# Chunk states and C-by-state products from high and low float32r parts in a hybrid pooling and SSD block

## The chip, the cores and the metric

The kernel runs on one core of a Trainium2 chip. The metric is the device time of one execution in microseconds (us), as the median of several runs. The engines of the core work side by side, each through its own queue of instructions in order: TensorE (PE) does matrix products into PSUM, VectorE (DVE), ScalarE (ACT) and GpSimd (POOL) do elementwise work, and SyncE (SP) starts DMA transfers; ACT and POOL can start them too.

## The reference

One decoder block for 1024 tokens of width 1024, in float32: an adaLN norm, one input projection that feeds a pooling mixer and a Mamba-2 mixer (SSD), an output projection with a gated residual, then a squared-ReLU MLP with its gated residual and a final norm. The change touches only the SSD mixer, which works in 8 chunks of 128 tokens, with 16 heads of 64 columns in two groups of 8:

```python
scores = jnp.einsum('bclgn,bcsgn->bclsg', cc, bc)
y_diag = jnp.einsum('bclsgr,bcsgrp->bclgrp', scores[..., None] * decay_in, xdt)
states = jnp.einsum('bclgn,bclgr,bclgrp->bcgrpn', bc, decay_out, xdt)
...
def step(h, inp):
    st, dec = inp
    return h * dec[..., None, None] + st, h
...
y_off = jnp.einsum('bclgn,bcgrpn,bclgr->bclgrp', cc, prev, jnp.exp(a_cum))
return (y_diag + y_off).reshape(Bsz, S, G, R, P)
...
y = y.reshape(Bsz, S, SSD_INNER) * jax.nn.silu(z.astype(jnp.float32))
```

So each chunk and group makes a state (B transposed times the weighted x), adds it to the decayed state of the chunks before, and the next chunk multiplies its C by that state. The gate z multiplies the mixer's output.

## The kernel before

All of it is float32 arithmetic. Large products are made from two parts of each operand: the high part is the value cast to float32r, the low part is the value less its high part, and `mm3` (L239 to L247) adds three float32r products, high by high, high by low and low by high. All of these products have line L247 in the profile, whoever called them. The weights come in units (`unit`, L187): SP loads `raw` (L193), ACT makes `hi` (L198), DVE makes `lo` (L199).

The stages in order of time: a start-up with the adaLN products; from about 70 us `z0_tok` (L595), which makes the first 240 gate columns and the step sizes dt for each of the 8 token tiles, where ACT writes `zt` (L600, two buffers) and DVE writes the result into `z0s` (L601), a tile that stays in SBUF until the mixer's end; then rounds of `feat`, 24 products into one bank of PSUM, each followed by a causal convolution (`conv_half`: ACT L556, L565, L571 and DVE three times L568, then L576 or L579), whose results PE turns into token order later (L141). From 152 to 228 us these rounds carry head group 0 of the SSD: after every `feat` one closure from the `side` queue is emitted. From 241 us the rounds of the pooling mixer (`pool_half`, DVE L804 and L808) and the first rounds of the remaining gate columns (`z_tok`, L898) carry group 1 in the same way.

The closure of chunk c, called a step here, does the following. `ssd_a(c)`: PE makes the scores (L715); ACT makes eight tiles of decays (L724) from `R` into `dec`, a tile with four buffers; DVE multiplies them by the scores (L725); `ssd_x` makes `xdt` on DVE (L701) and, on POOL, `xw` (L705, one buffer) and the skip term into `tok` (L707); PE turns B (L141) and ACT copies it to `btok` (L733). `ssd_r(c+1)`: SP loads `R` (L691) and POOL masks it (L693). `ssd_b(c-1)`: PE multiplies C by the state into the bank `po` (L743), makes eight products of 64 columns into `py` (L746), and makes the chunk's state from `btok` and `xw` into `pst_` (L750). Then POOL decays the running state in place (L756) and DVE adds the new one (L757), and DVE adds up the output (L758, L761, L763) and, in group 0, multiplies by the gate from `z0s` (L765).

L743 and L750 are plain float32 products: a state of 128 by 512 and one matmul instruction each, which appears as two records in the trace. The state of chunk c-1 must be complete before L743 of the next step, which stands one `feat` later in PE's queue.

A scheduler fixes the order within each engine's queue from the order of emission and the waits between instructions; nothing overtakes in a queue when the kernel runs. PSUM has eight banks, given out in turn (`bank`).

Of the kernel before, what the change touches and what calls it, by code (L numbers as in the profile page):

```python
# [13 lines left out]
ALU = mybir.AluOpType  # L14
# [58 lines left out]
def tile_hybrid_block(  # L73
# [58 lines left out]
    cum_d = dramp.tile([2 * NT, S], F32, name="cum_d")  # L132
    ypool_d = dramp.tile([4, P, S], F32, name="ypool_d")
    hres_d = [dramp.tile([P, D], F32, name=f"hres{t}") for t in range(NT)]
    f_d = [dramp.tile([P, 2, 7, HW], F32, name=f"f_d{q}") for q in range(8)]
# [407 lines left out]
    carry = {ct: mp.tile([P, 4], F32, name=f"carry{ct}") for _, ct in G0}  # L543
    z0s = mp.tile([P, NT, Z0], F32, name="z0s")
    dtr = mp.tile([P, NT, HEADS], F32, name="dtr")
# [49 lines left out]
    def z0_tok(t, ks):  # L595
        ps = bank()
        tok_mm(ps[:, :256], t, ks)
        dve.tensor_tensor(out=dtr[:, t, :], in0=ps[:, Z0:256], in1=dtb, op=ALU.add)
        th = accp.tile([P, 272], F32, name="zt", tag="zt", bufs=2)
        act.activation(out=th[:, :Z0], in_=ps[:, :Z0], func=AF.Tanh, scale=0.5)  # L600
        dve.scalar_tensor_tensor(out=z0s[:, t, :], in0=th[:, :Z0], scalar=1.0, in1=ps[:, :Z0],  # L601
                                 op0=ALU.add, op1=ALU.mult)

    def feat(ks, h):
# [34 lines left out]

    ax, e_, s_, cumt = (mp.tile([P, HW], F32, name="dec", tag="dec", bufs=4)[:, :P] for _ in range(4))  # L640
    xf = dtr.rearrange("p t h -> p (t h)")
# [37 lines left out]
    live = {}  # L679
    states = {}  # L680

    def hbc(t, c_, g, n):
# [5 lines left out]
    def ssd_r(g, c_):  # L688
        a = c_ * HEADS + g * 8
        R = mp.tile([P, 8, P], F32, name="R", tag="R", bufs=2)  # L690
        sp.dma_start(out=R.rearrange("p h l -> p (h l)"),  # L691
                     in_=cum_d[a // 8:a // 8 + 1, :].broadcast_to([P, S]))
        pool.affine_select(out=R, in_=R, pattern=[[0, 8], [1, P]], compare_op=ALU.is_ge, fill=-1e38, base=0,  # L693
                           channel_multiplier=-1)
        Rs[(g, c_)] = R
# [15 lines left out]
    def ssd_a(g, c_):  # L711
        B, C = BC[8 + g], BC[10 + g]
        cs = slice(c_ * P, (c_ + 1) * P)
        pscore = bank()
        pe.matmul(pscore[:, :P], lhsT=B[:, cs], rhs=C[:, cs], start=True, stop=True)  # L715
        sc = pscore[:, :P]
        Ms = []
        R = Rs.pop((g, c_))
        for b in range(2):
            dec = mp.tile([P, HW], F32, name="dec", tag="dec", bufs=4)  # L720
            dv = dec.rearrange("p (h l) -> p h l", l=P)
            for i in range(4):
                a = c_ * HEADS + g * 8 + b * 4 + i
                act.activation(out=dv[:, i, :], in_=R[:, 4 * b + i, :], func=AF.Exp, bias=ncum[:, a:a + 1])  # L724
            dve.tensor_tensor(out=dv, in0=dv, in1=sc.unsqueeze(1).broadcast_to([P, 4, P]), op=ALU.mult)  # L725
            Ms.append(dec)
        xdt, xw = ssd_x(g, c_)
        btok = None
        if c_ < NT - 1:
            pb = bank()  # L730
            turn(pb[:, :P], B[:, cs])
            btok = mp.tile([P, P], F32, name="btok", tag="btok", bufs=2)
            act.copy(btok, pb[:, :P])  # L733
        live[(g, c_)] = (Ms, xdt, xw, btok)

    def ssd_b(g, c_):
        Ms, xdt, xw, btok = live.pop((g, c_))
        C = BC[10 + g]
        cs = slice(c_ * P, (c_ + 1) * P)
        yv = tok[:, c_, g * 512:(g + 1) * 512]  # L740
        if c_ > 0:
            po = bank()
            pe.matmul(po, lhsT=C[:, cs], rhs=states[g], start=True, stop=True)  # L743
        py = bank()
        for hh in range(8):
            pe.matmul(py[:, hh * HD:(hh + 1) * HD], lhsT=Ms[hh // 4][:, (hh % 4) * P:(hh % 4 + 1) * P],  # L746
                      rhs=xdt[:, hh * HD:(hh + 1) * HD], start=True, stop=True)
        if c_ < NT - 1:
            pst_ = bank()
            pe.matmul(pst_, lhsT=btok, rhs=xw, start=True, stop=True)  # L750
            if c_ == 0:
                states[g] = mp.tile([P, HW], F32, name="state", tag="state", bufs=1)
                act.copy(states[g], pst_)
            else:
                sv = states[g].rearrange("p (h d) -> p h d", d=HD)
                pool.tensor_tensor(out=sv, in0=sv, in1=hbc(cdec, c_, g, HD), op=ALU.mult)  # L756
                dve.tensor_tensor(out=states[g], in0=states[g], in1=pst_, op=ALU.add)  # L757
        dve.tensor_tensor(out=yv, in0=yv, in1=py, op=ALU.add)  # L758
        if c_ > 0:
# [4 lines left out]
        if g == 0:  # L764
            dve.scalar_tensor_tensor(out=tok[:, c_, 0:Z0], in0=tok[:, c_, 0:Z0], scalar=0.5, in1=z0s[:, c_, :],  # L765
                                     op0=ALU.mult, op1=ALU.mult)

    def queue_ssd(g):
        ssd_r(g, 0)
        for c_ in range(NT):  # L770
            def one(c_=c_):
                ssd_a(g, c_)
                if c_ + 1 < NT:
                    ssd_r(g, c_ + 1)
                if c_ > 0:
                    ssd_b(g, c_ - 1)
            side.append(one)
        side.append(lambda: ssd_b(g, NT - 1))
# [859 lines left out]
```

## Time and profile before

| what | value |
|---|---|
| median of 3 runs | 1151.14 us (1151.13 to 1153.94) |
| the profiled execution, its own time | 1152.16 us |
| its span | 1150.5 us |
| TensorE clock granted, mean of the span | 0.997 |
| DVE busy | 822.2 us (71%) |
| ACT busy | 562.6 us (49%) |
| POOL busy | 148.2 us (13%) |

The profile describes one execution. A busy time is the union of an engine's instructions, and an engine that waits in the middle of an instruction counts as busy. The chain of waits is followed back from the last instruction, so its rows give, in order of time, what the end waited for; "x24" in a row is the number of records merged into it. Rows of the windows view give the busy time of each engine within a stretch of the span.

### The profile page before, as it was taken

How to read it: one execution, taken by the hardware profiler on the slowest of the kernel's cores; microseconds unless marked ns; L12 is line 12 of the kernel's file. 1: busy time of each engine (PE TensorE's matmuls, PEld its weight loads, DVE VectorE, ACT ScalarE, POOL GpSimd, SP SyncE). 2: the span in 40 equal slices, each digit the busy share in tenths (PEclk: the TensorE clock that was granted, in tenths of full speed). 3: DMA queues.
4: the chain of work that ended last, by engine and by line, in shares of the span. 5: the costliest groups of instructions: out<-in, count | busy, mean ns of one | idle time of the engine just before them, and what ended most of it. 6: DMA issues, size and time to landing. Idle time of an engine off the chain costs nothing.

```text
span 1150.5 us, 15234 instructions
## 1 busy us (share of the span) xinstructions
PE 1138.3 (99%) x5541; PEld 948.1 (82%) x5541; DVE 822.2 (71%) x1230; ACT 562.6 (49%) x985; POOL 148.2 (13%) x188
## 2 busy tenths in 40 slices
PE   9999999999999999999999999999999999999997
PEld 9889887877898888888788888888888888888886
DVE  4769989967878667666987666665458744586985
ACT  4477575544354424545774444444434344434373
POOL 3011335425400012022000000000100000000030
PEclk9999999999999999999999999999999999999999
DMA  9932432223256656863165434342599835775832
GB/s 280 254 114 64 131 92 83 93 86 115 74 183 188 226 191 229 257 198 114 36 238 192 174 134 168 143 160 88 211 382 345 308 94 162 254 238 196 279 116 90
DMA packets 123899, 200.72 MB, mean 174 GB/s; under 512 B 8464, under 2 KB 65584, under 8 KB 121776
## 3 DMA queue, kind: packets, MB, share of 16 engines
q1 hardware_dynamic: 122464, 196.24, 50.9%
q0 software_dynamic: 1120, 3.21, 0.9%
q8 instruction: 43, 0.70, 0.3%
q10 hardware_dynamic: 240, 0.30, 0.1%
q14 instruction: 32, 0.26, 0.1%
HBM read 159.81 MB, written 39.91 MB: 174 GB/s over the span
## 4 chain that ended last, share of the span: by engine, by line
PE 79%; DVE 7%; DMA 7%; ACT 2%; issue 2%; POOL 1%; POOLq 0%; SPq 0%; DVEq 0%; ACTq 0%
PE bank L247 70%; DMA raw<-in_w_ada_dram 4%; PE bank L746 2%; DVE acc L854 2%; DMA raw<-ypool_d 1%; DMA raw<-in_w_out_dram 1%; DVE lo L199 1%; PE bank L141 1%; PE bank L750 1%; PE bank L338 1%; PE bank L743 1%; PE bank L821 1%; POOL rst L183 1%; POOL tok L1001 0%; DVE wx L1179 0%
## 5 line engine op out<-in xcount | busy, mean ns | idle before, releaser
L247 PE MATMUL bank<-u,hi 128*128 128x512 f32 x560 | 182.6, 405 | 0.5 <-ACT u L390 0.4
L247 PE MATMUL bank<-dlo,dhi 128*128 128x512 f32 (+1 forms) x464 | 177.2, 382 | 0.0
L247 PE MATMUL bank<-dhi 128*128 128x512 f32 (+1 forms) x464 | 177.2, 382 | 0.0
L247 PE MATMUL bank<-dhi,dlo 128*128 128x512 f32 (+1 forms) x464 | 177.1, 382 | 0.0
L1457 ACT CAST dhi<-fr 128x1024 fp32r<-128x1024 f32 x56 | 58.9, 1052 | 142.8 <-PE bank L247 109.1
L247 PEld LDWEIGHTS bank<-u,hi 128*128 128x128 f32 x560 | 103.7, 189 | 26.6 <-issue 4.8
L1458 DVE TENSOR_TENSOR dlo<-fr,dhi 128x1024 fp32r<-128x1024 f32 x56 | 68.4, 1222 | 78.6 <-ACT dhi L1457 77.9
L247 PE MATMUL bank<-hi,ym 128*128 128x512 f32 x384 | 123.6, 395 | 0.0
L247 PE MATMUL bank<-u,lo 128*128 128x512 f32 x280 | 110.2, 393 | 0.0
L198 ACT CAST hi<-raw 128x512 fp32r<-128x512 f32 (+2 forms) x101 | 62.9, 634 | 80.2 <-DMA raw<-in_w_out_dram 41.6
L247 PEld LDWEIGHTS bank<-dlo,dhi 128*128 128x128 f32 x464 | 87.2, 188 | 17.0
L247 PEld LDWEIGHTS bank<-dhi,dlo 128*128 128x128 f32 x464 | 87.2, 188 | 17.0
L247 PEld LDWEIGHTS bank<-dhi 128*128 128x128 f32 x464 | 87.2, 188 | 16.8
L199 DVE TENSOR_TENSOR lo<-raw,hi 128x512 fp32r<-128x512 f32 (+2 forms) x101 | 75.1, 752 | 30.3 <-ACT hi L198 29.9
L247 PE MATMUL bank<-E,whl 128*128 128x512 f32 x384 | 92.7, 391 | 0.1
L247 PEld LDWEIGHTS bank<-E,whl 128*128 128x128 f32 x384 | 71.7, 188 | 16.6 <-DVE whl L1231 0.9
L247 PEld LDWEIGHTS bank<-hi,ym 128*128 128x128 f32 x384 | 72.1, 188 | 14.8 <-ACT hi L198 0.2
L183 POOL TENSOR_TENSOR rst<-ssq,mhalf 128x1 f32<-128x1 f32 (+2 forms) x27 | 26.5, 984 | 401.7 <-DVE ssq L182 368.2
L247 PE MATMUL bank<-u,whl 128*128 128x512 f32 x312 | 75.6, 389 | 0.0
L247 PE MATMUL bank<-lo,ym 128*128 128x512 f32 x192 | 74.9, 390 | 0.2 <-DVE lo L199 0.2
L247 PEld LDWEIGHTS bank<-u,whl 128*128 128x128 f32 x312 | 58.5, 188 | 12.5 <-DVE whl L1231 0.5
L1231 DVE TENSOR_TENSOR whl<-wraw,whl 128x512 fp32r<-128x512 f32 x58 | 39.9, 688 | 38.4 <-ACT whl L1226 38.3
(272 smaller groups left out, 2144.9 us busy)
## 6 DMA issues: line engine op xcount, KB each, us to landing
f_d<-tok SPq DMA_DIRECT2D x16, 1792.0 KB, 7.1
wr<-in_w_down_dram SPq DMA_DIRECT2D x56, 512.0 KB, 5.6
fr<-f_d SPq DMA_DIRECT2D x53, 512.0 KB, 4.8
raw<-in_w_ada_dram SPq DMA_DIRECT2D x64, 256.0 KB, 2.9
wraw<-in_w_up_dram SPq DMA_DIRECT2D x15, 1024.0 KB, 5.3
raw<-in_w_in_dram SPq DMA_DIRECT2D x48, 256.0 KB, 3.1
raw<-in_w_out_dram SPq DMA_DIRECT2D x48, 256.0 KB, 3.1
tok<-in_x_dram SPq DMA_DIRECT2D x16, 512.0 KB, 6.4
```

The lines of the kernel that those rows point to most:

```text
L141: return pe.transpose(dst, src, ident)
L183: pool.tensor_tensor(out=rst[:, a:b], in0=m, in1=mhalf[:, :b - a], op=ALU.pow)
L198: act.copy(hi[:, :n], raw[:, :n])
L199: dve.tensor_tensor(out=lo[:, :n], in0=raw[:, :n], in1=hi[:, :n].bitcast(F32), op=ALU.subtract)
L247: pe.matmul(ps, lhsT=st_, rhs=mv, start=first and i == 0, stop=last and i == 2, skip_group_check=more)
L338: pe.matmul(warm_ps[:, 0:P], lhsT=ones, rhs=ones, start=True, stop=True)
L743: pe.matmul(po, lhsT=C[:, cs], rhs=states[g], start=True, stop=True)
L746: pe.matmul(py[:, hh * HD:(hh + 1) * HD], lhsT=Ms[hh // 4][:, (hh % 4) * P:(hh % 4 + 1) * P], rhs=xdt[:, hh * HD:(hh + 1) * HD], start=Tru ...
L854: dve.scalar_tensor_tensor(out=acc[0], in0=raw, scalar=cact[:, k:k + 1], in1=acc[0], op0=ALU.mult, op1=ALU.add)
L1231: dve.tensor_tensor(out=t_[:, 1], in0=src, in1=t_[:, 0].bitcast(F32), op=ALU.subtract)
L1457: act.copy(hi, src)
L1458: dve.tensor_tensor(out=lo, in0=src, in1=hi.bitcast(F32), op=ALU.subtract)
```

## The change

Five edits, all in the SSD stage and in what feeds it.

1. L743 and L750 become `mm3` calls with float32r parts: `shl` (state), `chl` (C of the chunk), `xhl` (the weighted x) and `bhl` (B of the chunk), each with one buffer. `two_parts` makes them: the high part by an ACT copy, the low part by a POOL subtraction. Per chunk and group these are two pairs of 128x512 and two of 128x128, seven times each per group.
2. The state's parts are made at the end of `ssd_b`'s state update, those of x, B and C at the end of the closure.
3. The decays are written over `R`, and the `dec` tiles are gone; `R` has three buffers in place of two, and the small temporaries of the step sizes lie in one of them.
4. `btok` has one buffer in place of two.
5. `z0s` is gone: DVE writes the first gate columns over `zt`, POOL's queue stores them to DRAM (`z0_d`), and SP loads them again into `z0` (two buffers) one chunk before they are used.

```diff
+    z0_d = [dramp.tile([P, Z0], F32, name=f"z0_d{t}") for t in range(NT)]
...
-    z0s = mp.tile([P, NT, Z0], F32, name="z0s")
...
         act.activation(out=th[:, :Z0], in_=ps[:, :Z0], func=AF.Tanh, scale=0.5)
-        dve.scalar_tensor_tensor(out=z0s[:, t, :], in0=th[:, :Z0], scalar=1.0, in1=ps[:, :Z0],
+        dve.scalar_tensor_tensor(out=th[:, :Z0], in0=th[:, :Z0], scalar=1.0, in1=ps[:, :Z0],
                                  op0=ALU.add, op1=ALU.mult)
+        pool.dma_start(out=z0_d[t], in_=th[:, :Z0])
...
-    ax, e_, s_, cumt = (mp.tile([P, HW], F32, name="dec", tag="dec", bufs=4)[:, :P] for _ in range(4))
+    dts = mp.tile([P, 8, P], F32, name="R", tag="R", bufs=3)
+    ax, e_, s_, cumt = (dts[:, i, :] for i in range(4))
...
-        R = mp.tile([P, 8, P], F32, name="R", tag="R", bufs=2)
+        R = mp.tile([P, 8, P], F32, name="R", tag="R", bufs=3)
...
         for b in range(2):
-            dec = mp.tile([P, HW], F32, name="dec", tag="dec", bufs=4)
-            dv = dec.rearrange("p (h l) -> p h l", l=P)
+            dv = R[:, 4 * b:4 * b + 4, :]
             for i in range(4):
                 a = c_ * HEADS + g * 8 + b * 4 + i
-                act.activation(out=dv[:, i, :], in_=R[:, 4 * b + i, :], func=AF.Exp, bias=ncum[:, a:a + 1])
+                act.activation(out=dv[:, i, :], in_=dv[:, i, :], func=AF.Exp, bias=ncum[:, a:a + 1])
...
-            btok = mp.tile([P, P], F32, name="btok", tag="btok", bufs=2)
+            btok = mp.tile([P, P], F32, name="btok", tag="btok", bufs=1)
...
+    def low_part(v, src):
+        pool.tensor_tensor(out=v[:, 1, :], in0=src, in1=v[:, 0, :].bitcast(F32), op=ALU.subtract)
+
+    def two_parts(name, src, n=HW):
+        v = mp.tile([P, 2, n], F32R, name=name, tag=name, bufs=1)
+        act.copy(v[:, 0, :], src)
+        low_part(v, src)
+        return v
...
             po = bank()
-            pe.matmul(po, lhsT=C[:, cs], rhs=states[g], start=True, stop=True)
+            shl, chl = shls[g], chls.pop((g, c_))
+            mm3(po, shl[:, 0, :], shl[:, 1, :], (chl[:, 0, :], chl[:, 1, :]), True, True, False)
...
             pst_ = bank()
-            pe.matmul(pst_, lhsT=btok, rhs=xw, start=True, stop=True)
+            xp, bp = xhl.pop((g, c_))
+            mm3(pst_, xp[:, 0, :], xp[:, 1, :], (bp[:, 0, :], bp[:, 1, :]), True, True, False)
...
+            shls[g] = two_parts("shl", states[g])
...
+                if g == 0:
+                    z0r[c_] = mp.tile([P, Z0], F32, name="z0", tag="z0", bufs=2)
+                    sp.dma_start(out=z0r[c_], in_=z0_d[c_])
                 if c_ > 0:
                     ssd_b(g, c_ - 1)
+                if c_ < NT - 1:
+                    xhl[(g, c_)] = two_parts("xhl", live[(g, c_)][2]), two_parts("bhl", live[(g, c_)][3], P)
+                if c_ > 0:
+                    chls[(g, c_)] = two_parts("chl", BC[10 + g][:, c_ * P:(c_ + 1) * P], P)
```

On PE, a step of group 0 stands in the queue before the change as follows (`ct` and `bt` are C and B in feature order, `u` and `hi` the operands of the `feat` that comes next):

```order
L715 MATMUL bank<-ct,bt 128x128
L141 MATMUL bank<-ident,bt 128x128
L743 MATMUL bank<-state,ct 128x512
L746 MATMUL bank<-xdt,dec 128x64 x8
L750 MATMUL bank<-xw,btok 128x512
L247 MATMUL bank<-u,hi 128x512 x2
```

And the same step on PE after it:

```order
L721 MATMUL bank<-ct,bt 128x128
L142 MATMUL bank<-ident,bt 128x128
L248 MATMUL bank<-shl,chl 128x512 x3
L759 MATMUL bank<-xdt,R 128x64 x8
L248 MATMUL bank<-xhl,bhl 128x512 x3
L248 MATMUL bank<-u,hi 128x512 x2
```

Nothing moved on PE; two instructions of each step became three float32r products each.

On POOL, one step of group 0 with the small copies of the convolution behind it, before:

```order
L756 TENSOR_TENSOR state<-state,cdec 128x512
L705 TENSOR_TENSOR xw<-tok,wdt 128x512
L707 TENSOR_TENSOR tok<-tok,dsk 128x512
L693 AFFINE_SELECT R<-R 128x1024
L561 COPY car<-craw 128x3
L563 COPY craw<-car 128x3
```

And one step on POOL after it:

```order
L742 TENSOR_TENSOR chl<-ct,chl 128x128
L742 TENSOR_TENSOR xhl<-xw,xhl 128x512
L742 TENSOR_TENSOR bhl<-btok,bhl 128x128
L711 TENSOR_TENSOR xw<-tok,wdt 128x512
L742 TENSOR_TENSOR shl<-state,shl 128x512
L770 TENSOR_TENSOR state<-state,cdec 128x512
L699 AFFINE_SELECT R<-R 128x1024
L713 TENSOR_TENSOR tok<-tok,dsk 128x512
```

Four subtractions are new in the step; that of the state stands behind those of x and B and behind the next chunk's `xw`.

On ACT, one step of group 0 from the copy of B on, before:

```order
L733 COPY btok<-bank 128x128
L724 ACTIVATE dec<-R,ncum 128x128 x8
L571 ACTIVATE craw<-cv 128x512
L198 CAST hi<-raw 128x512 x2
L556 COPY craw<-bank 128x512
L585 COPY tok<-bank 128x4x128
L565 ACTIVATE cv<-craw,pw 128x512
```

And one step on ACT after it:

```order
L738 COPY btok<-bank 128x128
L746 CAST chl<-ct 128x128
L729 ACTIVATE R<-R,ncum 128x128
L199 CAST hi<-raw 128x512
L746 CAST xhl<-xw 128x512
L746 CAST bhl<-btok 128x128
L746 CAST shl<-state 128x512
L571 ACTIVATE craw<-cv 128x512
L729 ACTIVATE R<-R,ncum 128x128 x7
L556 COPY craw<-bank 128x512
L585 COPY tok<-bank 128x4x128
L565 ACTIVATE cv<-craw,pw 128x512
```

Four casts are new, and seven of the eight decays moved behind the cast of the state and behind the convolution's tanh (L571).

More of the change, by code (lines that the diff above doesn't have):

```diff
@@ L680, in tile_hybrid_block @@
     states = {}
+    shls = {}
+    z0r = {}
+    xhl = {}
+    chls = {}
     def hbc(t, c_, g, n):
@@ L719, in ssd_a @@
         for b in range(2):
-            dec = mp.tile([P, HW], F32, name="dec", tag="dec", bufs=4)
-            dv = dec.rearrange("p (h l) -> p h l", l=P)
+            dv = R[:, 4 * b:4 * b + 4, :]
             for i in range(4):
                 a = c_ * HEADS + g * 8 + b * 4 + i
-                act.activation(out=dv[:, i, :], in_=R[:, 4 * b + i, :], func=AF.Exp, bias=ncum[:, a:a + 1])
+                act.activation(out=dv[:, i, :], in_=dv[:, i, :], func=AF.Exp, bias=ncum[:, a:a + 1])
             dve.tensor_tensor(out=dv, in0=dv, in1=sc.unsqueeze(1).broadcast_to([P, 4, P]), op=ALU.mult)
-            Ms.append(dec)
+            Ms += [dv[:, i, :] for i in range(4)]
         xdt, xw = ssd_x(g, c_)
@@ L731, in ssd_a @@
             turn(pb[:, :P], B[:, cs])
-            btok = mp.tile([P, P], F32, name="btok", tag="btok", bufs=2)
+            btok = mp.tile([P, P], F32, name="btok", tag="btok", bufs=1)
             act.copy(btok, pb[:, :P])
         live[(g, c_)] = (Ms, xdt, xw, btok)
+    def low_part(v, src):
[5 more added lines that the diff above has]
+        return v
     def ssd_b(g, c_):
         Ms, xdt, xw, btok = live.pop((g, c_))
-        C = BC[10 + g]
-        cs = slice(c_ * P, (c_ + 1) * P)
         yv = tok[:, c_, g * 512:(g + 1) * 512]
@@ L742, in ssd_b @@
             po = bank()
-            pe.matmul(po, lhsT=C[:, cs], rhs=states[g], start=True, stop=True)
+            shl, chl = shls[g], chls.pop((g, c_))
+            mm3(po, shl[:, 0, :], shl[:, 1, :], (chl[:, 0, :], chl[:, 1, :]), True, True, False)
         py = bank()
         for hh in range(8):
-            pe.matmul(py[:, hh * HD:(hh + 1) * HD], lhsT=Ms[hh // 4][:, (hh % 4) * P:(hh % 4 + 1) * P],
+            pe.matmul(py[:, hh * HD:(hh + 1) * HD], lhsT=Ms[hh],
                       rhs=xdt[:, hh * HD:(hh + 1) * HD], start=True, stop=True)
@@ L764, in ssd_b @@
         if g == 0:
-            dve.scalar_tensor_tensor(out=tok[:, c_, 0:Z0], in0=tok[:, c_, 0:Z0], scalar=0.5, in1=z0s[:, c_, :],
+            dve.scalar_tensor_tensor(out=tok[:, c_, 0:Z0], in0=tok[:, c_, 0:Z0], scalar=0.5, in1=z0r.pop(c_),
                                      op0=ALU.mult, op1=ALU.mult)
```

## The prediction

> **What bounds the kernel now.** I read the busy times of the page first, then the windows over the SSD stage, then the chain of waits inside it.
>
> ```profile
> PE 1138.3 (99%) x5541; PEld 948.1 (82%) x5541; DVE 822.2 (71%) x1230; ACT 562.6 (49%) x985; POOL 148.2 (13%) x188
> ...
> 170.00:180.00 10.00, 10.00 (x56) 8.01 (x55) 10.00 (x13) 5.26 (x15) 6.45 (x7) 1.00 0.21 69
> 180.00:190.00 10.00, 10.00 (x55) 8.01 (x55) 9.84 (x15) 6.29 (x17) 5.03 (x5) 1.00 0.30 93
> 280.00:290.00 10.00, 10.00 (x50) 7.63 (x49) 8.34 (x14) 3.88 (x11) 5.53 (x6) 1.00 0.33 116
> 300.00:310.00 10.00, 10.00 (x66) 8.09 (x64) 9.17 (x16) 5.25 (x15) 5.62 (x6) 1.00 0.00 0
> ```
>
> The columns of a window are its length, then PE, weight loads, DVE, ACT and POOL busy. PE is busy all the time at clock 1.00, so time taken from PE's queue shortens the run, as long as nobody keeps PE waiting. But in group 0 (170 to 190 us) DVE is as full as PE: 10.00 and 9.84 of 10. POOL's share of 13% of the span says little here; in these windows it is 5 to 6.5 of 10.
>
> The chain of waits runs through PE alone in this stretch; its rows give start, length and the work:
>
> ```profile
> 177.67 0.86 PE bank L743 x2
> 178.53 1.73 PE bank L746 x16
> 180.26 0.91 PE bank L750 x2
> 181.18 5.49 PE bank L247 x24
> 186.66 0.44 PE bank L141 x4
> ...
> 187.43 0.86 PE bank L743 x2
> ```
>
> One step of group 0 is 9.76 us (177.67 to 187.43), without a gap. From the end of L750 (181.18) to the next L743 there are 6.25 us, in which the state must be brought up to date.
>
> **What the change takes from PE.** The two lines have these records in all:
>
> ```profile
> L743 PE MATMUL bank<-state,ct x28: 592/593/595, 167.7 to 315.6; 128*128 128x512 f32 x28
> L750 PE MATMUL bank<-xw,btok x28: 592/620/648, 161.0 to 311.8; 128*128 128x512 f32 x28
> ```
>
> At two records each, that is 14 products per line. The 592 and 620 ns are lengths of overlapping records; what counts in a queue is the pitch, 0.86 and 0.91 in the chain. A float32r product of the same shape has a pitch of 5.49 / 24 = 0.229, so three cost 0.68. I leave the 0.05 by which L750 exceeds L743 on the new form, since it sits between the short products and the next work, not in the form: 0.73. The gain is 14 x (0.86 - 0.68) + 14 x (0.91 - 0.73) = **5.0 us**; it is 5.7 if the 0.05 goes and 4.3 if both lines carry it. Per step it is 0.36, so PE's step falls to 9.40 us.
>
> **What it adds to POOL, and through POOL to DVE.** These are the groups of POOL in 163 to 226 us, then those of DVE in 163 to 223 us, with the sum and the mean of one behind the bar:
>
> ```profile
> L707 POOL TENSOR_TENSOR tok<-tok,dsk 128x512 f32<-128x512 f32 x7 | 9.7, 1381 | 1.1 <-DVE xdt L701 0.6
> L693 POOL TENSOR_SCALAR_AFFINE_SELECT R<-R 128x1024 f32<-128x1024 f32 x7 | 9.4, 1347 | 14.7 <-DMA R<-cum_d 14.7
> L705 POOL TENSOR_TENSOR xw<-tok,wdt 128x512 f32<-128x512 f32 x6 | 8.0, 1336 | 9.5 <-PE bank L750 9.5
> L756 POOL TENSOR_TENSOR state<-state,cdec 128x512 f32<-128x512 f32 x6 | 6.3, 1045 | 4.1 <-PE bank L743 4.0
> L563 POOL COPY craw<-car 128x3 f32<-128x3 f32 x3 | 0.6, 187 | 0.2
> ...
> L568 DVE SCALAR_TENSOR_TENSOR cv<-craw,pw,cv 128x512 f32<-128x512 f32 x20 | 18.1, 907 | 0.0
> L763 DVE TENSOR_TENSOR tok<-tok,y 128x512 f32<-128x512 f32 x5 | 5.1, 1018 | 0.0
> L757 DVE TENSOR_TENSOR state<-state,bank 128x512 f32<-128x512 f32 x6 | 4.1, 680 | 0.0
> ```
>
> L763 and L757 are the same DVE operation on the same shape, but L757 reads one operand from PSUM and takes 680 ns, and L763 reads both from SBUF and takes 1018. The timeline shows why:
>
> ```profile
> 181.26 1.37 POOL L705 TENSOR_TENSOR xw<-tok,wdt 128x512 f32<-128x512 f32 x1 [1.59 <-PE bank L750]
> 182.70 1.37 POOL L707 TENSOR_TENSOR tok<-tok,dsk 128x512 f32<-128x512 f32 x1
> ...
> 181.64 0.68 DVE L757 TENSOR_TENSOR state<-state,bank 128x512 f32<-128x512 f32 x1
> 182.24 0.94 DVE L568 SCALAR_TENSOR_TENSOR cv<-craw,pw,cv 128x512 f32<-128x512 f32 x1
> 183.10 0.68 DVE L761 TENSOR_TENSOR y<-bank,ea 128x512 f32<-128x512 f32 x1
> 183.70 0.93 DVE L701 TENSOR_TENSOR xdt<-tok,dt 128x512 f32<-128x512 f32 x1
> ```
>
> L568, begun while `xw` still ran on POOL, is stretched to 0.94 and ends 0.55 us after `xw` does; POOL's L707 then takes 1.37 where L756 takes 1.05, and L701 in turn is stretched to 0.93. L757 and L761, with an operand in PSUM, run beside POOL at 0.68. So a DVE operation with both operands in SBUF and a POOL operation take turns. From the end of `xw` (182.63) to that of L707 (184.07), 1.44 us, one of each went through; DVE's pitch is 0.60 (181.64 to 182.24), which leaves 0.84 for one of POOL's.
>
> The Trainium skill, page "SBUF — State Buffer", section "SBUF: two separate sides", states this as a rule: GpSimd and a DVE operation with two SBUF inputs share one port pair, an exclusive lock held for the whole instruction. The trace agrees (1018 against 680 ns), and this is a rule that speaks against moving the low parts to GpSimd; what it gives if nothing softens it is the second rival below.
>
> Per step of group 0 DVE has, by the code, seven such operations (L568 three times, L579, L763, L701, and L199 about once) and the shorter L765: 7 x 0.60 + 0.3 = 4.5 us. POOL has four large ones and small copies: 4 x 0.84 + 0.2 = 3.6. Together that is 8.1 of the 9.76 us. The change adds two subtractions of 128x512, for which I take 0.84, and two of 128x128, which the trace doesn't show on POOL: between 0.19 (L563) and a whole one's 0.84, I take 0.35, a fixed 0.19 and a quarter of the rest. That is 2 x 0.84 + 2 x 0.35 = 2.4, and the sum 10.5 us against PE's 9.40. DVE has no free time in which to hide it.
>
> Group 0 has six steps with the full load, so the bound from strict turn-taking is 6 x 1.1 = 6.6 us of waiting on PE; the bound from below is 0, if the work fits between PE's demands after all. Some is absorbed: the last step's mask and skip term (two of POOL's, 2 us) may finish after the group, and the state has a little slack, worked out next. I take **4.0 us**, near the upper end, because the DVE rows say full.
>
> The slack: at the end of L750 the new queue of POOL still has the low parts of x and B, the next `xw` and then that of the state. ACT's part of it is priced by these groups (the copy of B and a cast of the same size):
>
> ```profile
> L733 ACT COPY btok<-bank 128x128 f32<-128x128 f32 x7 | 1.8, 258 | 0.0
> L198 ACT CAST hi<-raw 128x512 fp32r<-128x512 f32 x37 | 22.6, 619 | 42.8 <-DMA raw<-in_w_out_dram 37.8 <-PE bank L247 4.9
> ```
>
> A cast is 0.62, then POOL 1.05 + 0.35 + 1.05 + 1.05 and four gaps of 0.07: 4.4 us, or 5.6 with two turns given to DVE, of the 6.25 us. DVE's addition (0.68) and the cast of the state lie beside it. ACT itself gains 2 x 0.62 + 2 x 0.26 = 1.8 us per step on 5 to 6 of 10 and isn't full; but seven decays now stand behind the cast of the state in its queue, so a late state also delays the decays, DVE's multiplication by them and PE's products after that.
>
> **Group 1.** Its middle steps are longer and its windows less full (DVE 8.34, POOL 5.53 of 10): adding 2.4 to 3.2 us of POOL's work nearly fills the step. I take 1.2 us for four of them; bounds 0 and 3.2 (four times the 0.8 by which a sum made as above, 4.3 + 3.6 + 2.4 = 10.3, and the hand-overs may exceed 9.8). At the end the `feat` is shorter:
>
> ```profile
> 297.06 0.91 PE bank L750 x2
> 297.97 2.99 PE bank L247 x24
> ...
> 301.29 0.86 PE bank L743 x2
> ...
> 303.88 0.91 PE bank L750 x2
> 304.79 2.99 PE bank L247 x24
> ...
> 308.86 0.86 PE bank L743 x2
> ```
>
> From L750's end to the next L743 there are only 3.32 and 4.07 us, where the chain just priced needs 4.4 to 5.6. PE waits 1.1 + 0.3 = 1.4 to 2.3 + 1.5 = 3.8 us; DVE is at 9.17 of 10 there, so I take 3.0. Group 1 then costs **4.2 us**, bounds 1.4 and 7.0.
>
> **The gate columns by DRAM.** `zt` has two buffers and is now free only when POOL's transfer has landed:
>
> ```profile
> dtb<-in_dt_bias_dram POOLq DMA_DIRECT2D x1, 8.0 KB, 5.3
> ...
> 95.75 0.40 DVE L601 SCALAR_TENSOR_TENSOR z0s<-zt,bank 128x240 f32<-128x240 f32 x1
> ...
> 99.72 0.35 ACT L600 ACTIVATE zt<-bank 128x240 f32<-128x240 f32 x1
> ...
> 100.00:120.00 20.00, 20.00 (x98) 16.66 (x97) 19.90 (x44) 15.05 (x29) 2.17 (x5) 1.00 0.40 106
> ```
>
> Tile 4 is written by 96.15; with 5.3 us to land and some 0.6 to issue it frees its buffer at 102.0, and tile 6's tanh wants it at 99.72. ACT and, behind it, DVE lose up to 2.3 us, and DVE is full until 120. PE is covered by three units of weights made ahead, so I take **0.5 us**, bounds 0 and 2.3. The eight loads on SP and the third buffer of `R` I cost at nothing: a load is issued a chunk ahead of its use, and weights lie three units ahead behind it. Without that cover a late load would hold up the weights in SP's queue. The decays in place issue nothing new.
>
> **The sum.** -5.0 + 4.0 + 4.2 + 0.5 = +3.7 us. Against the profiled run's own time (span 1150.5, with 1.7 around it 1152.16) that is 1155.9; the median of the runs lies 1.0 lower, so **1154.8 us**.
>
> **Rivals.** First, the low parts are hidden (against the forecast, not slower): POOL's subtractions fall where DVE works on PSUM operands, and the state's low part is ready within the 6.25 us. It decides at the price of POOL's chain, 4.4 us without a turn for DVE. Then only the 1.4 us of the short steps remain: -5.0 + 1.4 = -3.6, 1147.5 us. For it: PE shows no gap anywhere in the stage before. Against it: DVE at 10.00 of 10. Second, strict turn-taking with nothing absorbed: -5.0 + 6.6 + 7.0 + 2.3 = +10.9, 1162.0 us. For it: both engines were stretched in nearly every step; against it: before the change buffers carried DVE through a full window without a gap on PE. Third, the waits come to about the gain and nothing measurable is left, 1151 us: the absorbed part is as large as the excess.
>
> **Chances.** The forecast, 1152 to 1158, has 0.40; the hidden case 0.18; the strict case 0.25; the even case 0.17. The range is 1146.8 to 1162.0: it takes in the hidden case with most of the gain's own bounds and ends at the strict one. A measurement can tell 0.3%, 3.5 us, from no change, so faster begins below 1147.7 and slower above 1154.6: 0.18 faster (the hidden case), 0.32 the same (the even case and a third of the forecast's), 0.50 slower.
>
> **What would show it.** In the profile after, three records of some 0.23 pitch in place of 0.86 and 0.91 confirm the gain. The term of group 0 shows as PE waiting on its state product for POOL's low part of the state, and as means of L568 and L763's successors above 907 and 1018 ns, with POOL near 8 of 10; that of the short steps as waits at 300 to 310 us. The gate term shows as ACT waiting at `zt` for a transfer. I am wrong if PE has no gaps in 160 to 320 us, or if the gaps end on something else, such as the decays on ACT or a load on SP.

## The result, and the profile after

The changed kernel takes **1189.84 us** (median of 5 runs, 1188.76 to 1193.04), the kernel before 1151.14 beside it: a ratio of 1.033 (95% interval 1.031 to 1.035). The prediction was 1154.8 with a range up to 1162.0, so it was 35 us too low: +38.7 us in place of +3.7.

The page of the kernel after, with its busy times and, in 40 equal slices, the clock granted to PE in tenths:

```profile
PE 1154.5 (97%) x5569; PEld 969.3 (82%) x5569; DVE 856.1 (72%) x1230; ACT 582.5 (49%) x1041; POOL 215.1 (18%) x252
...
PEclk9999998799879999999999999999999999999999
```

PE is busy 16 us longer although it has less to do, its clock has slices of 8 and 7, and POOL has 67 us more than before. The windows of the SSD stage show how that hangs together (length, then PE, weight loads, DVE, ACT and POOL busy, then PE's clock):

```profile
180.00:190.00 10.00, 9.06 (x30) 7.86 (x31) 10.00 (x11) 5.91 (x16) 8.64 (x10) 0.52 0.28 91
190.00:200.00 10.00, 10.00 (x58) 8.58 (x57) 9.54 (x10) 5.55 (x15) 7.12 (x8) 1.00 0.10 25
200.00:210.00 10.00, 7.71 (x38) 6.65 (x37) 10.00 (x11) 4.79 (x14) 9.43 (x8) 0.83 0.23 67
320.00:330.00 10.00, 6.42 (x21) 5.13 (x22) 7.22 (x11) 3.95 (x12) 5.37 (x5) 0.50 0.07 26
```

Before, PE filled every window of this stage at clock 1.00. Now it has holes, and behind some of them the clock stands at about a half. Where in the steps the time lies is told by PE's timeline: the sixteen short products of a step (L746 before, L759 after) mark its pace. Rows give start, length and the work; those of the kernel before are the second and the eighth of group 0:

```profile
168.60 1.89 PE L746 MATMUL bank<-xdt,dec 128*128 128x64 f32 x16
...
226.72 1.89 PE L746 MATMUL bank<-xdt,dec 128*128 128x64 f32 x16
```

```profile
167.45 1.89 PE L759 MATMUL bank<-xdt,R 128*128 128x64 f32 x16
...
181.96 3.51 PE L759 MATMUL bank<-xdt,R 128*128 128x64 f32 x16
...
243.28 1.89 PE L759 MATMUL bank<-xdt,R 128*128 128x64 f32 x16
```

Six steps took 58.12 us (226.72 - 168.60), 9.69 each; now they take 75.83, 12.64 each. The same starts, read from the timelines of all kernels of this study that the text uses, give this table (us; "between" is from the last of group 0 to the first of group 1, the middle of group 1 its first four steps, "short" its last three):

| kernel | step of group 0 | six steps | between | group 1, middle | group 1, short |
|---|---|---|---|---|---|
| before | 9.69 | 58.12 | 27.84 | 40.60 | 20.90 |
| after | 12.64 | 75.83 | 30.58 | 53.49 | 28.19 |
| e4, float32 products | 9.69 | 58.12 | 29.10 | 41.01 | 20.97 |
| e6, e4 + unread subtractions | 12.27 | 73.63 | 35.79 | 50.37 | 23.19 |
| e16, e6 + decays behind | 10.84 | 65.04 | 28.57 | 44.80 | 24.84 |
| e9, after without y1 | 11.78 | 70.68 | 32.32 | 52.88 | 26.33 |
| e15, after + decays behind | 11.34 | 68.01 | 29.08 | 46.52 | 29.74 |
| e22, e15 without y1 | 10.45 | 62.72 | 28.44 | 44.89 | 29.06 |
| e2, after without low parts | 9.72 | 58.34 | 31.12 | 41.09 | 19.89 |
| e23, e2 + decays behind | 9.40 | 56.38 | 27.83 | 39.54 | 19.88 |

From the second step of group 0 to the end of group 1 the kernel after needs 188.1 us and the one before 147.5: the difference, 40.6 us, is the whole loss and a little more. The start-up with the gate columns costs nothing that shows (the second step begins at 167.45 where it began at 168.60).

What the engines wait for in 160 to 350 us (in all, times, longest):

```profile
ACT R L729 <- POOL R L699: 50.0, 13, 6.8
...
DVE psum L826 <- ACT craw L822: 19.5, 6, 8.8
POOL xhl L742 <- ACT xhl L746: 18.1, 10, 7.1
...
PE bank L843 <- issue: 9.9, 2, 7.1
PE bank L248 <- POOL shl L742: 9.3, 5, 3.1
```

Before, ACT never waited for POOL's mask of `R` there. Now that is the largest wait. What PE waits for is small beside it: the low part of the state, 9.3 us, and in group 1 the pooling mixer's product (L843), 9.9 us. For the second the profile names no releaser ("issue"), but its 7.1 us end at 323.58, just when DVE has made `pp` (L835, 322.43 to 323.48). DVE's `psum` in turn waits for ACT's copy `craw` (L822), which at 312.85 stands behind seven decays that had waited 6.48 us for the mask. The chain of waits through one step of group 0 shows how such a wait comes about:

```profile
182.43 2.15 ACT R L729 x7
...
185.53 0.72 ACT cv L565
186.90 0.63 ACT xhl L746
187.59 1.55 POOL xhl L742
189.15 0.86 POOL bhl L742
190.01 1.00 POOL xw L711
191.01 1.71 POOL shl L742
192.80 1.37 POOL state L770
194.17 1.51 POOL R L699
195.70 2.16 ACT R L729 x7
```

The mask ends at 182.43 and lets ACT do the decays; the convolution's `cv`, the casts, POOL's low parts, the next `xw`, the low part of the state and the update of the state follow, and behind them in POOL's queue stands the next mask, which ends at 195.70. One such **turn** is 13.3 us here, four of them (182.43 to 231.91) take 12.4 on average, near the step of 12.64, and PE isn't in it.

POOL's groups in 165 to 245 us (busy, mean ns of one, idle before):

```profile
L742 POOL TENSOR_TENSOR shl<-state,shl 128x512 fp32r<-128x512 f32 x7 | 11.2, 1596 | 3.0 <-ACT shl L746 3.0
...
L742 POOL TENSOR_TENSOR xhl<-xw,xhl 128x512 fp32r<-128x512 f32 x5 | 7.5, 1507 | 3.0 <-ACT xhl L746 3.0
...
L742 POOL TENSOR_TENSOR bhl<-btok,bhl 128x128 fp32r<-128x128 f32 x6 | 5.1, 858 | 0.0
L742 POOL TENSOR_TENSOR chl<-ct,chl 128x128 fp32r<-128x128 f32 x6 | 3.8, 635 | 9.3 <-ACT chl L746 9.3
```

And DVE's in 165 to 240 us:

```profile
L568 DVE SCALAR_TENSOR_TENSOR cv<-craw,pw,cv 128x512 f32<-128x512 f32 x19 | 18.6, 978 | 2.3 <-ACT cv L565 2.3
...
L778 DVE TENSOR_TENSOR tok<-tok,y 128x512 f32<-128x512 f32 x5 | 8.2, 1646 | 0.0
L730 DVE TENSOR_TENSOR R<-R,bank 128x512 f32<-128x512 f32 x12 | 7.6, 675 | 0.0
```

A low part of 128x512 occupies POOL for 1.5 to 1.6 us and one of 128x128 for 0.6 to 0.9. DVE's operations with both operands in SBUF went from 907 to 978 ns (L568) and from 1018 to 1646 (L778, which was L763), while L730, with one operand in PSUM, stays at 675.

### The profile page after: what moved, and what is told of

Same layout as the page of the kernel before. It is cut to its first block, busy times and chain, and to the rows that moved or that the text cites. A ratio compares the mean times of both kernels' runs of the same rounds, so it can differ in the third digit from the quotient of the medians.

```text
span 1188.2 us, 15455 instructions
## 1 busy us (share of the span) xinstructions
PE 1154.5 (97%) x5569; PEld 969.3 (82%) x5569; DVE 856.1 (72%) x1230; ACT 582.5 (49%) x1041; POOL 215.1 (18%) x252
## 4 chain that ended last, share of the span: by engine, by line
PE 70%; POOL 6%; ACT 6%; DVE 2%; issue 2%; DMA 1%; POOLq 0%; SPq 0%; ACTq 0%; DVEq 0%
PE bank L248 67%; ACT R L729 2%; POOL shl L742 1%; POOL R L699 1%; POOL xhl L742 1%; PE bank L759 1%; POOL xw L711 1%; DMA R<-cum_d 1%; PE bank L142 1%; ACT cv L565 1%; PE bank L843 0%; POOL bhl L742 0%; POOL state L770 0%; ACT xhl L746 0%; ACT craw L556 0%
## 5 line engine op out<-in xcount | busy, mean ns | idle before, releaser
L200 DVE TENSOR_TENSOR lo<-raw,hi 128x512 fp32r<-128x512 f32 (+2 forms) x101 | 82.5, 825 | 30.0 <-ACT hi L199 30.0
```

Of the source, the lines that this page charges most:

```text
L200: dve.tensor_tensor(out=lo[:, :n], in0=raw[:, :n], in1=hi[:, :n].bitcast(F32), op=ALU.subtract)
```

## The experiments

Two reasons stood first: the **loop theory** (the turn just shown sets the step) against the **full VectorE** or **load theory** (POOL's added time and DVE's turns with it set it). VectorE is DVE, GpSimd POOL, ScalarE ACT and TensorE PE in the expectations.

### Which of the edits

e4 puts the products back and keeps the rest of the change, but for `btok`, which has its two buffers again (in e6, e10, e12 and e16 too):

```diff
-            mm3(po, shl[:, 0, :], shl[:, 1, :], (chl[:, 0, :], chl[:, 1, :]), True, True, False)
+            pe.matmul(po, lhsT=BC[10 + g][:, c_ * P:(c_ + 1) * P], rhs=states[g], start=True, stop=True)
...
-            mm3(pst_, xp[:, 0, :], xp[:, 1, :], (bp[:, 0, :], bp[:, 1, :]), True, True, False)
+            pe.matmul(pst_, lhsT=btok, rhs=xw, start=True, stop=True)
```

> Changed kernel with the two products back in plain float32 (no casts, no low parts); first gate columns through DRAM, decays in place and three buffers of R stay. Loop and full VectorE theory alike: these edits cost nothing, 1149 to 1154 us. If the in-place decays or the loads of the gate columns carry a part of the loss: above 1160.

Measured: 1154.12 us, ratio 1.0008 (0.9992 to 1.0023). By themselves the gate columns through DRAM and the decays in place cost nothing. The single buffer of `btok` isn't in this run.

e6 adds to e4 four POOL subtractions in each step, at the places of the change, of the same sizes, into a tile that nobody reads:

```diff
+    def extra(a, b):
+        pool.tensor_tensor(out=xtra[:, :a.shape[1]], in0=a, in1=b, op=ALU.subtract)
...
+            extra(states[g], BC[8 + g][:, :HW])
```

> The kernel of the run before (float32 products) with GpSimd subtractions of the same four shapes and at the same four places a step, whose results nobody reads: the load on GpSimd and on the memory that it shares with VectorE is that of the change, but no cast stands before them and nobody waits for them. Loop theory: near the kernel without them, 1150 to 1158 us. Full VectorE theory: VectorE's two-operand instructions stretch by some 2.7 us a step in group 0 and less in group 1, 1168 to 1190 us.

Measured: 1187.02 us, ratio 1.029 (1.0258 to 1.0322). **Nearly the whole loss comes back with plain float32 products, no casts, and nobody reading the results.** The load theory's number held, and my loop, which ran through the casts, had predicted no loss. But e6's own chain shows a turn, of 12.4 us, without casts:

```profile
219.92 1.51 POOL R L699
221.46 2.17 ACT R L729 x7
224.57 0.72 ACT cv L565
...
226.64 0.74 DVE cv L568
227.38 0.61 DVE state L769
228.06 1.72 POOL xtra L784
...
232.31 1.51 POOL R L699
```

Mask, decays on ACT, `cv` behind them, DVE's convolution, DVE's new state behind that, POOL's subtraction that waits for that state, and behind it the next mask. An unread result still holds up what stands behind it in its queue.

### The order of the decays

What joins these queues is the place of the decays on ACT. The order of the two programs, with the numbers of buffers, at the fifth chunk of group 0 (its `R` is 2043 before and 2089 after; the copy and `cv` belong to the same half of the convolution in both):

```
before: L556 COPY craw_2002<-bank_1977 128x512
        L585 COPY tok_66<-bank_2014 128x4x128
        L565 ACTIVATE cv_2007<-craw_2002,pw_117 128x512
        L733 COPY btok_2041<-bank_2039 128x128
        L724 ACTIVATE dec_2111<-R_2043,ncum_825 128x128 x4
        L724 ACTIVATE dec_2117<-R_2043,ncum_825 128x128 x4
after:  L729 ACTIVATE R_2089<-R_2089,ncum_832 128x128 x7
        L556 COPY craw_2050<-bank_2025 128x512
        L585 COPY tok_66<-bank_2062 128x4x128
        L565 ACTIVATE cv_2055<-craw_2050,pw_125 128x512
        L738 COPY btok_2087<-bank_2085 128x128
```

Before, the decays needed one of four `dec` tiles and stood behind the convolution. In place, with a third buffer of `R`, they need only the mask, and the scheduler has put them ahead of the convolution, which now waits for the mask with them. (That the missing wait moved them is read from the order; no run undid this edit alone.) Three runs force the old place: e16 on e6, e15 on the kernel after, and e20, which puts the decays behind the casts of x and B as well.

```diff
+        marks.append(nc.cur_bb.bb.instructions[-1])      # cv in group 0, craw in group 1
...
                 act.activation(out=dv[:, i, :], in_=dv[:, i, :], func=AF.Exp, bias=ncum[:, a:a + 1])
+                tc.add_manual_dep(nc.cur_bb.bb.instructions[-1], marks[-2].name, ...)
```

> The kernel with float32 products and unread GpSimd subtractions, with one thing forced: on ScalarE a chunk's decays stand behind the convolution's three instructions (copy, token copy, cv) of the step before, as in the kernel before; with decays in place they had moved ahead of them. Every instruction stays. Order theory (mask behind GpSimd's instruction on the new state, decays behind the mask, convolution behind the decays on ScalarE, new state behind the convolution on VectorE: 12.3 us a turn): broken, 1150 to 1166 us. Load theory (GpSimd's added time and VectorE's turns with it are the limit): 1182 to 1191 us.

> The changed kernel with the decays on ScalarE forced behind the convolution's three instructions of the step before. Order theory: the turn over the convolution and the state is broken; the casts of xw and B still stand behind four to eight decays, so a turn over the cast of xw remains, about 11 us: 1155 to 1175 us. Load theory: 1184 to 1192 us.

> The changed kernel with the decays forced behind the convolution's instructions and behind the casts of C, xw and B of the chunk before. Order theory: no instruction of ScalarE that GpSimd waits for is behind the mask; only GpSimd's own 10.5 us a step is left, 1150 to 1168 us. Load theory: 1184 to 1192 us.

Measured: e16 1170.74 (ratio 1.0147, 1.0129 to 1.0164), e15 1176.38 (1.0194, 1.0174 to 1.0214), e20 1180.74 (1.0222, 1.0186 to 1.0259). All three lie between what the two theories gave. So the order is a cause: forcing it gives back 16 of e6's 33 us and, in e15, 13 to 16 of the 39. It is not the only one, and putting the decays further back gained nothing more. The scheduler also moved a few other instructions with the decays: PE's order is the same in e15 as in the kernel after, but on POOL the mask now stands more often ahead of the product that decays the state. So these 13 to 16 us belong to the forced order as a whole.

Two runs had tried to break the turn by moving the mask instead: e1 places it ahead of the low parts of C, x and B in POOL's queue, e10 gives e6 a fourth buffer of `R` and emits the masks one chunk earlier.

```diff
+                with pinned((pool,)):
+                    if c_ + 2 < NT:
+                        ssd_r(g, c_ + 2)
```

> Changed kernel, but GpSimd's mask of R for chunk c+2 is placed ahead of the low parts of chunk c in its queue (with three buffers of R its load then waits for chunk c-1's products). Loop theory (mask behind low parts behind casts behind decays behind mask, 13 us a turn): the loop is cut, the step falls from about 12.8 to what GpSimd's own work takes, 10.5 us, over some 12 steps: 1162 to 1172 us. Full VectorE theory (VectorE had 98% of each step before, and the low parts lengthen its two-operand instructions by 2.7 us a step): the same work remains, 1184 to 1192. Clock theory: if the PE waits stay, so does the half clock, 1184 to 1192; if they go, below 1165.

> The kernel with float32 products and unread GpSimd subtractions, with a fourth buffer of R, so that GpSimd's masks run one chunk further ahead; every instruction of GpSimd, VectorE, ScalarE and PE is kept. Loop theory, now without the casts (a GpSimd instruction that needs the new state stands ahead of the mask, the mask ahead of the decays on ScalarE, these ahead of the convolution that VectorE does before it makes the next state): a mask that is a chunk early breaks it, 1150 to 1162 us. Load theory (GpSimd's 10.5 us a step and VectorE's turns with it are themselves the limit): 1180 to 1191 us.

Measured: e1 1180.19 (1.0239, 1.0206 to 1.0272), e10 1186.12 (1.0302, 1.0276 to 1.0328). I first took e10 for the end of the loop theory. But in its order the scheduler had moved the decays one chunk ahead together with the masks, so that ACT still ran straight behind each mask: e10 didn't test what it was meant to, though its time is the load theory's. In e1 the mask still stood behind the low part of the state, and its time lies between what the two theories gave. Both are inconclusive.

### Half of the low parts

e11 keeps only the chunk states from parts, e12 only C by state, e13 has all of the change but makes the state's low part on DVE, and e21 is e11 with the decays behind the convolution and the casts.

> Changed kernel with only the chunk states from high and low parts (low parts of xw and of B, GpSimd); C by state is a plain float32 product. Loop theory: nothing ahead of the mask needs the state, the turn over the cast of xw takes 10.5 us or less, 1149 to 1160 us. Load theory: half of the added GpSimd work, half of the loss, 1166 to 1174 us.

> Changed kernel with only C by state from high and low parts (low parts of the state and of C, GpSimd); the chunk states are plain float32 products. Same number and sizes of GpSimd instructions as in the run with the chunk states only. Loop theory: the low part of the state stands ahead of the mask, so the loop over VectorE's state remains, 11 to 12 us a turn, 1166 to 1182 us, well above the other half. Load theory: the same as the other half, 1166 to 1174 us.

> Changed kernel with the low part of the state alone made by VectorE (0.68 us where L200 had no partner), the other three low parts by GpSimd. Loop theory: the state leaves GpSimd's queue, 1153 to 1166 us. Load theory: GpSimd loses one of its two long low parts, VectorE gets it, 1174 to 1186 us.

> The kernel with only the chunk states from high and low parts, with the decays forced behind the convolution's instructions and behind the casts of xw and B. Order theory: 1146 to 1153 us, the kernel before less half of TensorE's 5 us or level with it. Load theory: no better than without the forced order, 1163 to 1169 us.

Measured: e11 1167.66 (1.0143, 1.0119 to 1.0167), e12 1171.89 (1.0187, 1.0159 to 1.0216), e13 1177.36 (1.023, 1.0202 to 1.0258), e21 1155.94 (1.0034, 1.0014 to 1.0053). Either half of the low parts brings about half of the loss, and e13 too lies where the load theory had it. Yet in e11 the order makes most of that half: e21 does all that e11 does and is 1.1% of the time, 12 us, nearer to the kernel before, where the load theory saw no change. It ends some 3 us above the range of the order theory.

### DVE's work, alone and with the order

e9 takes 2.2 us of DVE's work from each step (`y1` and its addition), e22 does so in e15, and e3 gives all low parts to DVE.

```diff
-            dve.tensor_tensor(out=y1.rearrange("p (h d) -> p h d", d=HD),
-                              in0=po.rearrange("p (h d) -> p h d", d=HD), in1=hbc(ea, c_, g, HD), op=ALU.mult)
-            dve.tensor_tensor(out=yv, in0=yv, in1=y1, op=ALU.add)
+            dve.tensor_copy(out=y1[:, 0:4], in_=po[:, 0:4])
```

> Changed kernel without VectorE's product of C by state with ea and without its addition to the token values (L776, L778: the contribution of earlier chunks is left out of the result), 0.68 and 1.49 us of VectorE a step; a copy of four columns frees the bank. GpSimd, ScalarE and PE do all they did. Loop theory: these are not in the loop, 1183 to 1191 us. Full VectorE theory: each step falls by about 2.2 us, fourteen times, 1158 to 1170 us.

> The changed kernel with both edits that alone gave little: the decays on ScalarE behind the convolution's instructions, and VectorE without the product of C by state with ea and its addition (the contribution of earlier chunks is left out of the result). Two-limits theory (the turn through GpSimd, ScalarE and VectorE's state, 12.5 us, and VectorE's own stretched step, 11.6 us, both stand above TensorE's 9.4 us, so that lifting one shows the other): together they give far more than the 13 and 3 us of each alone, 1147 to 1158 us. GpSimd's own time as the limit: 1168 to 1176 us, the sum of the two at best.

> The changed kernel with all four low parts made by VectorE instead of GpSimd (quiet 0.68 us for 128x512, some 0.2 for 128x128: 1.8 us a step). Two-limits theory: GpSimd is back at its time of before and the turn over it is short, but VectorE, which had 0.2 us of a step free, gets 1.8 us, in group 0 alone some 1.4 us a step over and less in group 1: 1158 to 1172 us. If GpSimd's time alone is the limit: 1146 to 1152 us.

Measured: e9 1186.44 (1.0292, 1.0263 to 1.0322), e22 1168.60 (1.0151, 1.0132 to 1.017), e3 1176.28 (1.0215, 1.0192 to 1.0238). The step of group 0 gives back 0.86 us of the 2.2 in the one order (12.64 to 11.78) and 0.89 in the other (11.34 to 10.45). So DVE isn't the limit that the full VectorE theory took it for, and my idea of two limits of which one hides the other falls too, since the two edits simply add up. e22's chain runs mostly through POOL:

```profile
191.66 1.45 POOL state L775
193.15 0.83 POOL chl L747
...
196.11 1.00 POOL xw L714
197.11 1.84 issue
...
198.99 1.45 POOL shl L747
...
203.35 1.04 POOL state L775
```

From `state` at 191.66 to the next `state` at 203.35 it is 11.7 us. e22's time is what its expectation gave for GpSimd's own time as the limit (1168 to 1176 us), but that reason isn't shown: the 1.84 us that the chain calls "issue" are a wait. POOL's timeline of e22 names what ended it, and the group of the same instruction in e15 (165 to 240 us) has six of them with 10.6 us of idle time before them:

```profile
198.99 1.45 POOL L747 TENSOR_TENSOR shl<-state,shl 128x512 fp32r<-128x512 f32 x1 [1.88 <-ACT shl L751]
```

```profile
L747 POOL TENSOR_TENSOR shl<-state,shl 128x512 fp32r<-128x512 f32 x6 | 8.2, 1360 | 10.6 <-ACT shl L751 10.6
```

So POOL waits for ACT's cast of the state, and that cast (198.29 in e22) had waited 3.81 us for DVE's new state (L776, 197.59), which stands in DVE's queue behind two instructions of the convolution of 1.01 and 1.35 us (0.74 for the third). So read, POOL makes DVE's state late, and the late state makes POOL wait: the two set the step together. In e22, with less work on DVE, such waits of POOL add up to 6.8 us in 160 to 350 us; in e15 they are 12.7. And e3, with POOL's load gone and 1.8 us more on DVE, has steps of 11.93 and a time above both of its expected ranges, so DVE could not have taken the low parts either.

One window of 165 to 235 us of e15, and then of e22, shows how little a busy share tells here:

```profile
165.00:235.00 70.00, 65.78 (x332) 55.53 (x330) 69.77 (x78) 40.66 (x103) 56.57 (x56) 0.90 0.25 77
```

```profile
165.00:235.00 70.00, 66.22 (x358) 55.97 (x357) 69.63 (x82) 42.39 (x105) 60.83 (x59) 0.98 0.29 88
```

DVE is at 69.8 of 70 us in the one and at 69.6 in the other, though 2.2 us were taken from each of its steps: an instruction that waits for its turn with POOL counts as busy.

### Without the low parts

e2 drops the four subtractions and lets the products take the high parts twice; e23 is the same with the decays behind the convolution.

```diff
-        low_part(v, src)
...
-            mm3(po, shl[:, 0, :], shl[:, 1, :], (chl[:, 0, :], chl[:, 1, :]), True, True, False)
+            mm3(po, shl[:, 0, :], shl[:, 0, :], (chl[:, 0, :], chl[:, 0, :]), True, True, False)
```

> The changed kernel without the four subtractions on GpSimd; the products take the high parts twice, so that TensorE and ScalarE do what they did (the low parts of state, C, xw and B are left out of the result). Two-limits theory: GpSimd is back at its time of before, VectorE is no longer stretched, and the casts alone hold nobody up, 1145 to 1151 us. If the casts on ScalarE are a part of the loss: above 1156 us.

> The changed kernel without the four subtractions (products take the high parts twice, the low parts are left out of the result) and with the decays forced behind the convolution's instructions: the most that the shorter products can bring, if low parts cost nothing. If the order ate TensorE's 5 us in the run without low parts: 1145 to 1148 us. If VectorE, with 98% of a step of group 0, lets no shorter step pass there: only group 1 can gain, 1148 to 1152 us.

Measured: e2 1154.07 (1.0031, 1.0017 to 1.0044), e23 1146.99 (0.996, 0.9947 to 0.9974). e2 lies between its two expected ranges: the casts and PE's shorter products alone, in the new order, are no gain; in the old order they bring 4.6 us. That is PE's 5.0 within the interval, and the long steps of group 0, 9.76 us before, take 9.40. PE's and POOL's instructions stand in the same order in both runs, so the difference between them, 8 us, is the order on ACT and what moved with it on DVE and SP. DVE reads as full as ever in e23 (60 us of it):

```profile
165.00:225.00 60.00, 60.00 (x336) 51.66 (x335) 59.42 (x76) 38.99 (x100) 31.07 (x32) 1.00 0.30 90
```

### PE's halved clock

e26 puts the sixteen short products ahead of the product of C by state, so that PE has work where it waited.

```diff
+        with pinned((pe,)):
+            py = bank()
...
+            if c_ > 0:
+                po = bank()
```

> The changed kernel with TensorE's sixteen short products of a step forced ahead of the product of C by state, so that TensorE has 1.73 us of work where it waited for the state's low part. Two-limits theory: other engines set the step, TensorE's waits and the halved clock after them are hidden, 1184 to 1192 us. Clock theory (a wait of 3 us costs 3 to 10 us more at a granted clock of 0.5): fewer halved stretches and 1165 to 1180 us.

Measured: 1189.91 us (1.0335, 1.0308 to 1.0363). Two windows of the kernel after, then the same of e26 (PE's clock is the figure behind the five engines):

```profile
160.00:250.00 90.00, 82.02 (x389) 69.51 (x388) 86.21 (x96) 50.49 (x127) 64.66 (x62) 0.87 0.28 82
270.00:350.00 80.00, 67.76 (x328) 56.68 (x326) 55.95 (x77) 33.02 (x90) 52.36 (x49) 0.85 0.21 68
```

```profile
160.00:250.00 90.00, 79.78 (x408) 67.14 (x407) 87.35 (x101) 51.43 (x131) 62.09 (x63) 0.92 0.28 82
270.00:350.00 80.00, 68.56 (x343) 57.14 (x341) 58.42 (x82) 32.93 (x90) 51.04 (x48) 0.89 0.24 75
```

The clock rose from 0.87 to 0.92 and from 0.85 to 0.89: of 90 and 80 us, by estimate, 23.7 us had been lost to it (0.13 x 90 + 0.15 x 80) and now 16.0 are, and the time stayed. So far as this run shows, PE's slow stretches are a follower here: they fill time in which others set the step.

No kernel of these that takes a product from high and low parts, with all of the work in it, beats the kernel before; e21 comes nearest, 0.3% above it.

## Why the prediction was wrong

- **PE's gain, -5.0 us: right.** Three records in place of two, and 9.40 us for the long steps, as predicted; e23 shows -4.6 (-3.0 to -6.1).
- **"The decays in place issue nothing new", cost 0: the step that failed first.** They issue nothing, but they lost their wait for a `dec` tile, and with it their place behind the convolution. The prediction quoted the new order, read it as decays moved *behind* the cast of the state, and named a late state that delays the decays, without asking what stands behind the decays. They were the next chunk's, moved *ahead* of the convolution. The order costs nothing with float32 products (e4), 8 us with casts and no low parts (e2 less e23, 1.0031 - 0.996), and 16 us with low parts (after less e15, 1.0332 - 1.0194). The other part of the error is larger: the low parts themselves cost 27 us in the old order (e15 less e23, 1.0194 - 0.996), where 8.2 were counted, 4.0 for group 0 and 4.2 for group 1.
- **The slack of the state: right as a sum, wrong as a question.** POOL's 4.4 to 5.6 us of 6.25 were priced as one pass. The mask at the end of that pass and the decays that need it make it a turn, and a turn is compared with the step: 12.4 on average against 9.40.
- **Group 0, +4.0 (bounds 0 and 6.6).** Against the 56.38 us of e23 the six steps took 19.4 more. From after to e15 the order is 7.8 of them (75.83 - 68.01), and e15's 11.6 over e23 are the low parts themselves, with a step of 11.34 us. The prediction counted 10.5 for strict turn-taking and called it an upper bound. It left out that POOL's queue has waits of its own, above all that for the cast of a state which DVE brings late (10.6 us in e15's group 0), and that DVE's operations on PSUM, five with a pitch of 0.6 us a step, stand in the same queue as those that take turns: which falls beside which isn't free to choose. e22, with two of DVE's operations less, still takes 10.45. That POOL and DVE hold each other up in e15 and e22 is read from their traces; no run shortened one of their instructions without taking it away.
- **The small low parts, 0.35 us each: mis-sized.** They occupied POOL for 0.64 and 0.86 us with the waits for their turns in them, the large ones for 1.5 to 1.6 where 0.84 was counted without.
- **Group 1, +4.2 (bounds 1.4 and 7.0).** Against e23 its middle took 14.0 more and its short steps 8.3, and the stretch between the groups 2.8, for which there was no term. "Windows less full" was the reason for 1.2 in the middle; a turn doesn't ask how full a window is. The order is 5.4 of the 22.3 (81.68 - 76.26); how the rest divides between POOL's time, the casts that still stand behind decays there, and the pooling mixer's `pp` that PE waits for isn't settled.
- **"DVE has no free time", from 10.00 of 10: a wrong reading.** It led to the right engine pair, but e23 runs a step of 9.40 where it was 9.69, with DVE at 59.42 of 60. The Trainium skill, page "Perfetto Trace Analysis", section "Identifying the Most-Contended Engine", takes the engine with the highest occupancy as the one to work on first; e9 did that and came from 1.033 to 1.029 of the time, two values whose intervals overlap, so here the rule led to little.
- **The gate columns, +0.5: nothing.** POOL's transfers landed in 2.3 us, not 5.3:

```profile
z_d<-zt POOLq DMA_DIRECT2D x8, 120.0 KB, 2.3
```

- **The rivals.** Strict turn-taking came nearest in kind and was 28 us short: no rival held the order, and with the old order e15 is still 14 us above it. The markers named (PE waiting for the state's low part, longer L568 and L778, POOL at 8 of 10) all appeared. The decays on ACT, which were named as a sign of being wrong, don't end PE's gaps directly; they have the largest wait of all engines in front of them.

## What to carry to other kernels

When an edit takes a wait away, ask the order what moves up into its place, chunk by chunk with the numbers of buffers, and follow the engine's queue from there round to the same instruction of the next step: the length of that turn, not the share of busy time, is to be compared with the step. An instruction whose result nobody reads can cost as much as any other if a mask that others need stands behind it in its queue. A busy share near 10 of 10 on an engine that takes turns with another is no proof of a limit; take some of its work away and see how much of it the step gives back.

## What the runs showed that was not expected

PE's clock fell to a half after waits of only 1.5 to 3.1 us in the middle of work. Three rows of PE's timeline of the kernel after, with the wait and what ended it in brackets:

```profile
180.94 1.22 PE L248 MATMUL bank<-shl,chl 128*128 128x512 f32 x2 [3.12 <-POOL shl L742]
...
206.40 1.01 PE L248 MATMUL bank<-shl,chl 128*128 128x512 f32 x2 [2.29 <-POOL shl L742]
...
230.43 1.11 PE L248 MATMUL bank<-shl,chl 128*128 128x512 f32 x2 [1.48 <-POOL shl L742]
```

After each of them the sixteen short products, 1.89 us at full clock, took 3.51. The Trainium skill, page "TensorE: Matmul & The Clock Gate", section "Why this matters for your kernels", asks for no gaps above some 3 us; here 1.5 was enough. The length of one wait doesn't decide it alone: after 2.52 us before 259.60 the clock stayed (1.00 in the window from 260 to 270 us). And giving back 7.7 us of the lost clock in e26 changed the time by nothing.
